# A fp32 hybrid decoder trunk on one core: first unit by pairs of feature tiles, substitution on GpSimd, gated rows at other ticks

## The chip, the cores and the metric

The kernel runs on one core of a Trainium2 chip, as one program. The metric is the device time of one execution in microseconds (us). The engines are named as in the profile: PE is TensorE (PEld its weight loads), DVE is VectorE, ACT is ScalarE, POOL is GpSimd, SP is SyncE.

## The reference, cut to what matters

Two layers on 256 tokens of width 1024, batch 1, all in float32. Each layer is half a SwiGLU feed-forward, a token mixer, cross-attention to 256 memory tokens and another half feed-forward, each behind an RMS norm. The first layer's mixer is windowed attention beside a linear recurrence; the second layer's is a gated DeltaNet of 8 heads of 128 in chunks, which needs the inverse of a unit triangular matrix for each chunk and head.

```python
def rmsnorm(x, g):
    return x * rsqrt(mean(x * x) + 1e-6) * g

def swiglu(h, w_in, w_out):
    gate, up = split(h @ w_in, 2)
    return (silu(gate) * up) @ w_out

for l in range(2):
    x = x + 0.5 * swiglu(rmsnorm(x, ffn1_norm[l]), ffn1_w_in[l], ffn1_w_out[l])
    x = x + mixer[l](rmsnorm(x, mix_norm[l]))           # l = 1: gated DeltaNet
    x = x + cross_attention(rmsnorm(x, xa_norm[l]), mem)
    x = x + 0.5 * swiglu(rmsnorm(x, ffn2_norm[l]), ffn2_w_in[l], ffn2_w_out[l])

# gated DeltaNet, per head and chunk: q, k, v through a causal convolution of four taps
# and silu; decay g = -exp(a_log) * softplus(a + dt_bias); c = cumsum(g)
A = tril(beta * (k @ k.T) * exp(c[:, None] - c[None, :]), -1)
T = inverse(I + A)            # by substitution
# u = T @ (beta v), w = T @ (beta exp(c) k); state from chunk to chunk; output gated by silu(z)
```

## The kernel before, in words

**Units.** The work is a list of products of activations by 256 columns of a weight matrix, 1024 rows deep: a *unit*. A unit's weights come as two *halves* of four 128-row tiles, 512 KB each, loaded by SP (`load_to`, L141) into one of five `raw` buffers. A half is split (`split_half`) into a high part (ACT copies it, rounded, L158) and a low part (DVE subtracts that from the original, L159), both in `wt`, of which four buffers hold two units. Each unit has two output groups of 128 columns. A group is eight high matmuls (L200, 512 moving columns: high and low activations) and eight low matmuls (L204, 256 columns), into one of three result banks `psw`, read back by ACT and DVE (L270, L271). So a bank is free again when DVE has done L271 for the group three before.

**What sets the order.** Each engine runs its instructions in one order, fixed at build time, and waits at the head of it. Outside the first units a scheduler makes that order from the order in which the code issues work. The code issues it in *ticks*: generators of work are advanced by `run`, and after each step `tick` splits the next half when a unit needs it, pops one step that was put off, adds one to `now`, and runs what `after(n, fn)` has made due. Tables of tick counts say when the steps of the DeltaNet mixer (`mixer1`) come: `EXP` for the exponentials of the decay, `INV` for the substitution, and others.

**The first units** are written out by hand under a manual schedule in `setup`. SP issues a norm's rows, then x in four pieces (feature tiles in pairs), with the first halves between. TensorE runs products of ones (`idle`), transposes x by pairs (L429), and ACT and DVE split the transposed x into high (L503) and low (L506). Then the products of units 0 and 1 follow by halves.

**The DeltaNet mixer.** Its units are, in this order: 'k0 k1 q0 q1 k2 v0 k3 v1 z0', then 'v3 z1 v2 q2' behind a first back substitution, 'q3', and 'z2 z3 K2 K3' behind the second. A unit such as k2 gives two heads (a *pair*, p = 0 to 3) of keys; DVE runs the convolution taps (`y`, L1081). The decay rows pass through memory (`gd`) and come back as `e` by POOL's transfers L1126, and ACT takes 16 exponentials (L1132), four a pair. DVE then makes the entries of the triangular blocks, `na` (L1176), which SP stores (L1180). For two pairs at a time (group 0: pairs 0, 1; group 1: pairs 2, 3) `invert` takes the 16 x 16 diagonal blocks back as `nb` (L1235), 64 of them side by side, and substitutes in 15 steps of a product (L1240) and a sum (L1242), on DVE. The finished blocks `ti` are copied transposed (L1244), stored (L1248) and read back spread over the partitions as `tu` (L1254); the function `back` goes on with products L1275 to L1287.

Small powers run on POOL (L341): `rs_dn` for the scale of keys and queries. The sums they need are products with ones on TensorE (L1110). L1204 is the product of keys and queries.

Of the kernel before, what the change touches and what calls it, by code (L numbers as in the profile page):

```python
# [9 lines left out]
F32 = mybir.dt.float32  # L10
# [3 lines left out]
AF = mybir.ActivationFunctionType  # L14
# [4 lines left out]
P = 128  # L19
S = 256  # L20
D = 1024
KD = 8
# [45 lines left out]
class Net:  # L68
    def __init__(self, tc, t):
        self.tc, self.nc, self.t = tc, tc.nc, t  # L70
        self.raws, self.halves = {}, {}
        self.plan = list(self.make_plan())
        self.queue = [(i, k) for i, u in enumerate(self.plan) for k in range(0, u[4], 4)]

        self.queue[1], self.queue[2] = self.queue[2], self.queue[1]
        self.n_load = self.n_half = self.n_take = 0
        self.later = deque()
        self.banks, self.n_bank = "w", 0
        self.now, self.due = 0, []
# [46 lines left out]
            yield from four("xa_wo", l)  # L126
            yield from ffn(2, l)

    def load_to(self, n, step=4):

        nc = self.nc
        while self.n_load < min(n, len(self.queue)):
            i, k = self.queue[self.n_load]
            name, l, c0, k0, nk, cols = self.plan[i]
            m = min(4, nk - k)
            raw = self.p_raw.tile([P, 4, 256], F32, name="raw")
            src = self.t[name][l, (k0 + k) * P:(k0 + k + m) * P, c0:c0 + cols]
            src = src.rearrange("(k p) c -> p k c", p=P)
            for u in range(0, m, step):
                us = slice(u, min(m, u + step))  # L140
                nc.sync.dma_start(raw[:, us, :cols], src[:, us])  # L141
            self.raws[self.n_load] = raw
            self.n_load += 1

    def split_half(self, step=4):

        nc = self.nc
        i, k = self.queue[self.n_half]
        name, l, _, _, nk, cols = self.plan[i]
        self.load_to(self.n_half + 1)  # L150
        n = min(4, nk - k)
        wt = self.p_wt.tile([P, 4, 2, 256], F32R, name="wt")
        raw = self.raws.pop(self.n_half)
        self.n_half += 1
        for u in range(0, n, step):
            us = slice(u, min(n, u + step))
            a, b, r = wt[:, us, 0, :cols], wt[:, us, 1, :cols], raw[:, us, :cols]
            nc.scalar.activation(a, r, AF.Copy)  # L158
            nc.vector.tensor_sub(b, r, a.bitcast(F32))  # L159
        self.halves.setdefault(i, []).append(wt)  # L160

    def w(self, name, c0):

# [23 lines left out]

    def mm3(self, out, wts, cols, mov, ks, k0=0, start=0, stop=KD):  # L190

        nc = self.nc
        for k in ks:
            i = k - k0
            w = wts[i // 4][:, i % 4]

            def high():
                nc.tensor.matmul(out.rearrange("p a s -> p (a s)"), w[:, 0, cols], mov[:, k].rearrange("p a s -> p (a s)"),  # L200
                                 start=k == start, stop=k == stop - 1)

            def low():
                nc.tensor.matmul(out[:, 0], w[:, 1, cols], mov[:, k, 0], start=False, stop=False)  # L204

            for part in (low, high) if k == stop - 1 else (high, low):
                part()

# [223 lines left out]
    def setup(self, ctx):  # L432
        nc, tc, t = self.nc, self.tc, self.t
# [20 lines left out]
        self.dcw = c.tile([P, P], F32, name="dcw")  # L454

        warm = c.tile([P, 1], F32, name="warm")
        nc.scalar.activation(warm, self.ones[:, :1], AF.Silu)
        x_pool = tc.tile_pool(name="xs", bufs=1, reuse_waits="tile")
        xs = x_pool.__enter__().tile([P, 2, D], F32, name="xs")
        x = t["x"][0].rearrange("(t p) d -> p t d", p=P)  # L460
        spare = self.p_sm.tile([P, S], F32, name="acc", bufs=2)
        rows0, rows, rows2 = self.dcw, spare[:, :P], spare[:, P:]

# [3 lines left out]
            eng.dma_start(dst[r0:r0 + n * times],  # L467
                          bass.AP(tensor=ap.tensor, offset=ap.offset, ap=[[0, times], [P, n], [1, P]]))

        put(rows0, 0, "ffn1_norm", nc.sync, times=8)  # L470

        for a, b in ((0, 256), (256, 512)):
            nc.sync.dma_start(xs[:, :, a:b], x[:, :, a:b])
        self.load_to(1, 2)
        self.load_to(2)
        for a, b in ((512, 768), (768, 1024)):
            nc.sync.dma_start(xs[:, :, a:b], x[:, :, a:b])
        self.load_to(RAW)
        xs = [xs[:, j] for j in range(2)]

# [5 lines left out]
        with tc.manual_schedule():  # L486

            def idle(n):
                ps = self.bank("w").rearrange("p a s -> p (a s)")
                for _ in range(n):  # L490
                    nc.tensor.matmul(ps[:, :P], self.ones, self.ones, start=True, stop=True)

            idle(7)
            gains = self.p_sm.tile([P, 1, S], F32, name="bc", bufs=2)[:, 0, :P]
            columns(gains, rows0, "w")
            banks = []

            def take(ks, ps):
                banks.append((ks, ps))
                g = lambda k: gains[:, C_FFN1 + k:C_FFN1 + k + 1]  # L500
                for j in range(2):
                    k = ks.start + j
                    nc.scalar.activation(self.x2[:, k, 0], ps[:, j], AF.Copy, scale=g(k))  # L503
# [8 lines left out]
            def products(u, half, j):  # L512
                self.mm3(self.first[u][j], self.halves[u], slice(j * P, j * P + P), self.x2,
                         range(4 * half, 4 * half + 4))

            self.transposed(xs, take, (0,))
            idle(3)
            self.transposed(xs, take, (1,))
            idle(6)
            self.split_half(2)  # L520
            products(0, 0, 0)
            self.split_half()
            products(0, 0, 1)
            self.transposed(xs, take, (2, 3))
            products(1, 0, 0)
            products(1, 0, 1)
            for u in range(2):
                self.split_half(2)
                for j in range(2):
                    products(u, 1, j)  # L530
# [477 lines left out]
    def mixer1(self, mid, kT_mem, mem_mov, gnext):  # L1008
# [4 lines left out]
        with tc.tile_pool(name="m1", bufs=1, reuse_waits="tile") as mp:  # L1013
# [213 lines left out]
            def invert(g):  # L1227
# [9 lines left out]

                def step(j):
                    n, m = 15 - j, j + 1
                    nc.vector.tensor_mul(tm[:, :n, :m], nb[:, j, m:, None].to_broadcast([64, n, m]),  # L1240
                                         ti[:, 0, j:m, :m].to_broadcast([64, n, m]))
                    nc.vector.tensor_add(ti[:, 0, m:, :m], ti[:, 0, m:, :m], tm[:, :n, :m])  # L1242
                    if j == 14:
                        nc.vector.tensor_copy(ti[:, 1], ti[:, 0].rearrange("p a b -> p b a"))  # L1244

# [147 lines left out]
            for i, part in enumerate(DN_ORDER):  # L1393
                if i % 2 == 0:
                    for step in part.split():
                        self.run(unit(step))
                    continue
                group, bg = part.split("|")
                gens = [back(int(p)) for p in group]
                bg = deque(unit(step) for step in bg.split())  # L1400
                parts = list(DN_FILL[i // 2])
                if i == 1:
                    self.fill(bg, 2)
                while gens:
                    gens = [g_ for g_ in gens if next(g_, 0) is None]
                    if gens:
                        self.fill(bg, parts.pop(0))
                if i == 1:
                    self.fill(bg)
                    for n, p in enumerate(group):  # L1410
                        self.after(1 + n, lambda p=int(p): gated(p))
                        self.after(4 + n, lambda p=int(p): gated_T(p))
                    continue
                for p in group:
                    gated(int(p))
                for p in group:
                    self.fill(bg, parts.pop(0))
                    gated_T(int(p))
                self.fill(bg)
# [81 lines left out]
```

## Time and profile before

| | us |
|---|---|
| median of 3 runs | 1252.54 (1251.08 to 1254.22) |
| profiled execution, its own time | 1250.74 |
| its span, first to last instruction | 1249.0 |
| TensorE busy | 1235.7 |
| VectorE busy | 929.3 |
| ScalarE busy | 751.8 |
| GpSimd busy | 80.9 |

The mean clock granted to TensorE was 0.999 of full speed. In rows of the profile, L12 is line 12 of the kernel; a tile's name is that of the program without its number. A row of the timeline gives the start in us, the time, engine, line, operation, output and inputs, shapes, how many operations are joined, and in brackets the idle time before it and what ended it. Busy time of different engines overlaps. SPq marks SP's issue of a transfer, not the transfer.

### The profile page before, as it was taken

The numbers are of one execution on the slowest core, as the hardware profiler recorded it, in microseconds if no ns is written. First come the engines' busy times: TensorE is split into PE (matmuls) and PEld (weight loads), VectorE is DVE, ScalarE is ACT, GpSimd is POOL, SyncE is SP. The second block draws the span as 40 slices with busy tenths as digits, with TensorE's granted clock in tenths as the row PEclk, the third lists the DMA queues.
The fourth block names the chain that finished last, engine by engine and source line by source line (L and its number), as shares of the span: only waits on it lengthen the run. The fifth ranks groups of instructions, "written<-read, shape, count | busy, mean of one in ns | idle before, by whom it ended". The sixth has DMA issues, their size and how long they took to land.

```text
span 1249.0 us, 20308 instructions
## 1 busy us (share of the span) xinstructions
PE 1235.7 (99%) x7702; PEld 1105.1 (88%) x7702; DVE 929.3 (74%) x1594; ACT 751.8 (60%) x1281; POOL 80.9 (6%) x97
## 2 busy tenths in 40 slices
PE   9999999999999999999999999999999999999998
PEld 8888889888998888888888888888898998888887
DVE  6987957788668778766877756989757668777753
ACT  7766545886555665545666544776757555665543
POOL 1000020000101000011000001020001101000000
PEclk9999999999999999999999999999999999999999
DMA  8766575534544565556656566667533545566552
GB/s 272 215 208 197 185 254 185 177 128 151 187 135 153 185 195 184 187 183 229 188 185 198 175 193 206 189 150 197 140 102 132 178 131 165 185 190 188 177 188 72
DMA packets 231018, 222.92 MB, mean 178 GB/s; under 512 B 14968, under 2 KB 228616, under 8 KB 230792
## 3 DMA queue, kind: packets, MB, share of 16 engines
q1 hardware_dynamic: 229448, 217.94, 55.9%
q0 software_dynamic: 1152, 3.15, 1.0%
q8 instruction: 60, 0.98, 0.3%
q10 hardware_dynamic: 320, 0.53, 0.1%
q14 instruction: 38, 0.31, 0.1%
HBM read 215.03 MB, written 5.51 MB: 177 GB/s over the span
## 4 chain that ended last, share of the span: by engine, by line
PE 90%; DVE 5%; ACT 2%; DMA 1%; issue 1%; POOL 1%; ACTq 0%; DVEq 0%; POOLq 0%
PE psw L200 21%; PE pss L200 16%; PE psw L204 11%; PE psf L200 11%; PE pss L204 8%; PE psf L204 5%; PE psw L242 5%; PE psf L242 4%; PE pss L242 3%; PE psw L216 2%; DVE wt L159 1%; PE psw L220 1%; ACT wt L158 1%; PE pss L1275 1%; PE psf L1281 1%
## 5 line engine op out<-in xcount | busy, mean ns | idle before, releaser
L159 DVE TENSOR_TENSOR wt<-raw,wt 128x1024 fp32r<-128x1024 f32 (+1 forms) x409 | 484.6, 1190 | 203.3 <-ACT wt L158 200.5
L158 ACT ACTIVATE wt<-raw 128x1024 fp32r<-128x1024 f32 (+1 forms) x409 | 418.6, 1031 | 172.3 <-PE psw L204 59.4
L200 PE MATMUL psw<-x,wt 128*128 128x512 f32 x864 | 310.6, 396 | 1.7 <-DVE xn L271 1.5
L204 PE MATMUL psw<-x,wt 128*128 128x256 f32 x864 | 224.9, 281 | 0.5 <-DVE wt L159 0.5
L200 PE MATMUL pss<-x,wt 128*128 128x512 f32 x520 | 187.4, 393 | 0.0
L200 PEld LDWEIGHTS psw<-x,wt 128*128 128x128 f32 x864 | 160.6, 188 | 29.7 <-issue 1.7
L204 PEld LDWEIGHTS psw<-x,wt 128*128 128x128 f32 x864 | 162.5, 188 | 9.4 <-DVE wt L159 1.0
L204 PE MATMUL pss<-x,wt 128*128 128x256 f32 x520 | 134.9, 280 | 0.0
L200 PE MATMUL psf<-x,wt 128*128 128x512 f32 x352 | 127.2, 394 | 0.0
L200 PEld LDWEIGHTS pss<-x,wt 128*128 128x128 f32 x520 | 97.7, 188 | 16.9 <-ACT bc L377 0.4
L204 PEld LDWEIGHTS pss<-x,wt 128*128 128x128 f32 x520 | 97.7, 188 | 5.4
L200 PE MATMUL psw<-h,wt 128*128 128x512 f32 x264 | 94.9, 396 | 0.0
L204 PE MATMUL psf<-x,wt 128*128 128x256 f32 x352 | 91.3, 280 | 0.0
L200 PE MATMUL pss<-h,wt 128*128 128x512 f32 x242 | 87.0, 396 | 0.0
L336 POOL TENSOR_TENSOR acc<-acc,sq 128x256 f32<-128x256 f32 x49 | 43.7, 891 | 658.5 <-ACT sq L334 557.5
L200 PEld LDWEIGHTS psf<-x,wt 128*128 128x128 f32 x352 | 66.1, 188 | 11.2
L204 PE MATMUL psw<-h,wt 128*128 128x256 f32 x264 | 72.0, 280 | 0.0
L204 PEld LDWEIGHTS psf<-x,wt 128*128 128x128 f32 x352 | 66.2, 188 | 3.5
L204 PE MATMUL pss<-h,wt 128*128 128x256 f32 x242 | 66.0, 280 | 0.0
L200 PEld LDWEIGHTS psw<-h,wt 128*128 128x128 f32 x264 | 49.6, 188 | 10.8
L200 PE MATMUL psf<-h,wt 128*128 128x512 f32 x154 | 55.4, 397 | 0.0
L200 PEld LDWEIGHTS pss<-h,wt 128*128 128x128 f32 x242 | 45.5, 188 | 9.8
(385 smaller groups left out, 2108.9 us busy)
## 6 DMA issues: line engine op xcount, KB each, us to landing
raw<-in_ffn_w_in_dram SPq DMA_DIRECT2D x175, 512.0 KB, 3.6
raw<-in_ffn_w_out_dram SPq DMA_DIRECT2D x80, 512.0 KB, 3.5
raw<-in_xa_wkv_dram SPq DMA_DIRECT2D x32, 512.0 KB, 3.4
raw<-in_dn_w_in_dram SPq DMA_DIRECT2D x32, 512.0 KB, 4.0
raw<-in_ab_w_in_dram SPq DMA_DIRECT2D x20, 512.0 KB, 3.5
raw<-in_xa_wq_dram SPq DMA_DIRECT2D x16, 512.0 KB, 3.5
raw<-in_xa_wo_dram SPq DMA_DIRECT2D x16, 512.0 KB, 3.3
raw<-in_ffn_w_out_dram SPq DMA_DIRECT2D x16, 256.0 KB, 2.7
```

Of the source, the lines that this page charges most:

```text
L158: nc.scalar.activation(a, r, AF.Copy)
L159: nc.vector.tensor_sub(b, r, a.bitcast(F32))
L200: nc.tensor.matmul(out.rearrange("p a s -> p (a s)"), w[:, 0, cols], mov[:, k].rearrange("p a s -> p (a s)"), start=k == start, stop=k == ...
L204: nc.tensor.matmul(out[:, 0], w[:, 1, cols], mov[:, k, 0], start=False, stop=False)
L216: nc.tensor.matmul(out.rearrange("p a s -> p (a s)"), mov[:, k, 0, tok], w.rearrange("p a s -> p (a s)"), start=k == 0, stop=k == KD - 1)
L220: nc.tensor.matmul(out[:, 0], mov[:, k, 1, tok], w[:, 0], start=False, stop=False)
L242: self.nc.tensor.matmul(out, a[u], b[w], start=first and i == 0, stop=last and i == 2)
L336: (eng or nc.gpsimd).tensor_add(self.acc, self.acc, sq)
L1275: nc.tensor.matmul(py[:, i], na[:, i], tu[:, 0, i], start=True, stop=True)
L1281: nc.tensor.matmul(pp[:, i], yy[:, i], tu[:, 1, i], start=True, stop=True)
```

## The change: what it does

It has four parts.

1. In the first unit, x and the weights are loaded alternately in pairs of feature tiles (`load_pair`), the norm's rows go to ACT's queue, the products of unit 0 go by pairs of tiles (four highs, then four lows), and the weights are split by pairs between the pieces of x. Eight idle products go.
2. The substitution's product and sum go from DVE to POOL. The copy behind them stays on DVE.
3. The gated rows and their transposes are put off by 2 + n and 6 + n ticks, not 1 + n and 4 + n.
4. `split_half` hands the splitting to `run`, as a generator. `run` calls `tick` after each step, so a split is a tick of its own: a unit in the steady part counts six ticks, before it counted four. The tables `EXP`, `INV` and the others keep their numbers.

```diff
-        self.queue[1], self.queue[2] = self.queue[2], self.queue[1]
...
+    def load_pair(self, n):
+        name, l, c0, _, _, cols = self.plan[0]
+        if n % 2 == 0:
+            self.raws[n // 2] = self.p_raw.tile([P, 4, 256], F32, name="raw")
+        src = self.t[name][l, 2 * n * P:(2 * n + 2) * P, c0:c0 + cols].rearrange("(k p) c -> p k c", p=P)
+        self.nc.sync.dma_start(self.raws[n // 2][:, 2 * n % 4:2 * n % 4 + 2, :cols], src)
+        self.n_load = n // 2 + 1
...
-    def split_half(self, step=4):
+    def split_half(self):
+        self.run(self.split_steps(4))
+
+    def split_steps(self, step):
...
             nc.scalar.activation(a, r, AF.Copy)
             nc.vector.tensor_sub(b, r, a.bitcast(F32))
-        self.halves.setdefault(i, []).append(wt)
+            yield
...
-        put(rows0, 0, "ffn1_norm", nc.sync, times=8)
-
-        for a, b in ((0, 256), (256, 512)):
-            nc.sync.dma_start(xs[:, :, a:b], x[:, :, a:b])
-        self.load_to(1, 2)
-        self.load_to(2)
-        for a, b in ((512, 768), (768, 1024)):
-            nc.sync.dma_start(xs[:, :, a:b], x[:, :, a:b])
+        put(rows0, 0, "ffn1_norm", nc.scalar, times=8)
...
+        for n in range(4):
+            nc.sync.dma_start(xs[:, :, n * 256:n * 256 + 256], x[:, :, n * 256:n * 256 + 256])
+            self.load_pair(n)
...
-            idle(7)
+            idle(5)
...
+            w0 = weights()
             self.transposed(xs, take, (0,))
             idle(3)
-            self.transposed(xs, take, (1,))
-            idle(6)
-            self.split_half(2)
-            products(0, 0, 0)
-            self.split_half()
-            products(0, 0, 1)
-            self.transposed(xs, take, (2, 3))
...
+            next(w0)
+            for n in range(3):
+                self.transposed(xs, take, (n + 1,))
+                products(0, range(2 * n, 2 * n + 2), late=True)
+                next(w0)
+            products(0, range(6, 8))
+            for half in range(2):
+                self.split_half()
+                products(1, range(4 * half, 4 * half + 4))
...
-                    nc.vector.tensor_mul(tm[:, :n, :m], nb[:, j, m:, None].to_broadcast([64, n, m]),
+                    nc.gpsimd.tensor_mul(tm[:, :n, :m], nb[:, j, m:, None].to_broadcast([64, n, m]),
                                          ti[:, 0, j:m, :m].to_broadcast([64, n, m]))
-                    nc.vector.tensor_add(ti[:, 0, m:, :m], ti[:, 0, m:, :m], tm[:, :n, :m])
+                    nc.gpsimd.tensor_add(ti[:, 0, m:, :m], ti[:, 0, m:, :m], tm[:, :n, :m])
...
-                        self.after(1 + n, lambda p=int(p): gated(p))
-                        self.after(4 + n, lambda p=int(p): gated_T(p))
+                        self.after(2 + n, lambda p=int(p): gated(p))
+                        self.after(6 + n, lambda p=int(p): gated_T(p))
```

Where the change moves instructions, the rows of the new order have the new program's line numbers, eleven or twelve above the old in the mixer (L1143 is the old L1132, L1255 the old L1244, L283 the old L271, L168 the old L159).

TensorE at the start of the program, before (L491 idle products of ones, L483 the norm's rows, L429 transposes of x, L200 and L204 high and low products):

```order
1 L491 MATMUL psw<-ones 128x128 x7
2 L483 MATMUL psw<-ident,dcw 128x128
3 L429 MATMUL psf<-ident,xs 128x128 x4
4 L491 MATMUL psw<-ones 128x128 x3
5 L429 MATMUL pss<-ident,xs 128x128 x4
6 L491 MATMUL psw<-ones 128x128 x6
7 L200 MATMUL psw<-x_79,wt 128x512
8 L204 MATMUL psw<-x_79,wt 128x256
```

and now:

```order
1 L500 MATMUL psw<-ones 128x128 x5
2 L492 MATMUL psw<-ident,dcw 128x128
3 L441 MATMUL psf<-ident,xs 128x128 x4
4 L500 MATMUL psw<-ones 128x128 x3
5 L441 MATMUL pss<-ident,xs 128x128 x4
6 L209 MATMUL psw<-x_79,wt 128x512 x4
7 L213 MATMUL psw<-x_79,wt 128x256 x4
8 L441 MATMUL psf<-ident,xs 128x128 x4
```

The first products stand right behind the second transposes, four highs and then four lows, and the next transposes stand between pairs.

ScalarE around the exponentials of the decay (e), in the units q1 and k2 of the mixer, before (th is the tanh or square of a finished convolution, xn the read of a result bank, wt a half's split):

```order
691 L158 ACTIVATE wt<-raw 128x4x256
692 L1078 ACTIVATE y<-xn,dcw 128x256
693 L1132 ACTIVATE e<-e,ngc 128x128 x3
694 L1087 ACTIVATE th<-y 128x512
695 L270 ACTIVATE xn<-psw 128x256
696 L1132 ACTIVATE e<-e,ngc 128x128 x3
697 L1104 ACTIVATE th<-y 128x512
```

and now:

```order
690 L1089 ACTIVATE y<-xn,dcw 128x256
691 L1143 ACTIVATE e<-e,ngc 128x128 x8
692 L1098 ACTIVATE th<-y 128x512
693 L282 ACTIVATE xn<-psw 128x256
694 L1143 ACTIVATE e<-e,ngc 128x128 x3
695 L1115 ACTIVATE th<-y 128x512
696 L1209 ACTIVATE q_8265<-y 128x256
697 L1089 ACTIVATE y<-xn,dcw 128x256
698 L1143 ACTIVATE e<-e,ngc 128x128 x5
699 L282 ACTIVATE xn<-psw 128x256
700 L167 ACTIVATE wt<-raw 128x4x256
```

Eight exponentials in a row stand ahead of the first th, and the split of v0's second half, which stood ahead of all exponentials, stands behind them.

VectorE around the copy of the finished blocks of group 0, in the new order (y taps of the convolution, wt splits of halves, ti the blocks):

```order
944 L1099 SCALAR_TENSOR_TENSOR y<-th,y 128x512
945 L1092 SCALAR_TENSOR_TENSOR y<-xn,dcw,y 128x254
946 L283 TENSOR_TENSOR xn<-psw,xn 128x256
947 L1092 SCALAR_TENSOR_TENSOR y<-xn,dcw,y 128x253
948 L1255 COPY ti<-ti 64x256
949 L168 TENSOR_TENSOR wt<-raw,wt 128x4x256
950 L1092 SCALAR_TENSOR_TENSOR y<-xn,dcw,y 128x255
951 L1124 TENSOR_SCALAR ss<-pss 128x4
952 L1092 SCALAR_TENSOR_TENSOR y<-xn,dcw,y 128x254
953 L283 TENSOR_TENSOR xn<-psw,xn 128x256
```

In the order before, the copy stood behind the split of v3's first half, four splits later, with the thirty operations of the substitution interleaved ahead of it; now it stands ahead of the split of v1's first half and of the eviction of v0's first result, and waits for GpSimd's thirty operations.

More of the change, by code (lines that the diff above doesn't have):

```diff
@@ L127, in make_plan, with load_to @@
             yield from ffn(2, l)
-    def load_to(self, n, step=4):
+    def load_pair(self, n):
[5 more added lines that the diff above has]
+        self.n_load = n // 2 + 1
+    def load_to(self, n):
         nc = self.nc
@@ L138, in load_to @@
             src = src.rearrange("(k p) c -> p k c", p=P)
-            for u in range(0, m, step):
-                us = slice(u, min(m, u + step))
-                nc.sync.dma_start(raw[:, us, :cols], src[:, us])
+            nc.sync.dma_start(raw[:, :m, :cols], src)
             self.raws[self.n_load] = raw
             self.n_load += 1
-    def split_half(self, step=4):
+    def split_half(self):
+        self.run(self.split_steps(4))
+    def split_steps(self, step):
         nc = self.nc
@@ L154, in split_half @@
         self.n_half += 1
+        self.halves.setdefault(i, []).append(wt)
         for u in range(0, n, step):
@@ L186, in after, with mm3 @@
         self.due.sort(key=lambda e: e[:2])
-    def mm3(self, out, wts, cols, mov, ks, k0=0, start=0, stop=KD):
+    def mm3(self, out, wts, cols, mov, ks, k0=0, start=0, stop=KD, only=""):
         nc = self.nc
@@ L204, in low @@
                 nc.tensor.matmul(out[:, 0], w[:, 1, cols], mov[:, k, 0], start=False, stop=False)
+            if only:
+                (high if only == "high" else low)()
+                continue
             for part in (low, high) if k == stop - 1 else (high, low):
@@ L456, in setup @@
         warm = c.tile([P, 1], F32, name="warm")
[L457 to L460, printed above, removed]
         spare = self.p_sm.tile([P, S], F32, name="acc", bufs=2)
@@ L468, in put @@
                           bass.AP(tensor=ap.tensor, offset=ap.offset, ap=[[0, times], [P, n], [1, P]]))
-        put(rows0, 0, "ffn1_norm", nc.sync, times=8)
-        for a, b in ((0, 256), (256, 512)):
-            nc.sync.dma_start(xs[:, :, a:b], x[:, :, a:b])
-        self.load_to(1, 2)
-        self.load_to(2)
-        for a, b in ((512, 768), (768, 1024)):
-            nc.sync.dma_start(xs[:, :, a:b], x[:, :, a:b])
+        put(rows0, 0, "ffn1_norm", nc.scalar, times=8)
+        nc.scalar.activation(warm, self.ones[:, :1], AF.Silu)
+        x_pool = tc.tile_pool(name="xs", bufs=1, reuse_waits="tile")
+        xs = x_pool.__enter__().tile([P, 2, D], F32, name="xs")
+        x = t["x"][0].rearrange("(t p) d -> p t d", p=P)
+        for n in range(4):
+            nc.sync.dma_start(xs[:, :, n * 256:n * 256 + 256], x[:, :, n * 256:n * 256 + 256])
+            self.load_pair(n)
         self.load_to(RAW)
@@ L510, in setup, with products, weights @@
             self.first = [[self.bank(w) for w in u] for u in ("ww", "ws")]
-            def products(u, half, j):
-                self.mm3(self.first[u][j], self.halves[u], slice(j * P, j * P + P), self.x2,
-                         range(4 * half, 4 * half + 4))
+            def products(u, ks, late=False):
+                js = [slice(j * P, j * P + P) for j in range(2)]
+                for which in ("high", "low") if late else ("",):
+                    for j in range(2):
+                        self.mm3(self.first[u][j], self.halves[u], js[j], self.x2, ks, only=which)
+            def weights():
+                for _ in range(2):
+                    yield from self.split_steps(2)
+            w0 = weights()
             self.transposed(xs, take, (0,))
             idle(3)
-            self.transposed(xs, take, (1,))
-            idle(6)
-            self.split_half(2)
-            products(0, 0, 0)
-            self.split_half()
-            products(0, 0, 1)
-            self.transposed(xs, take, (2, 3))
[L525 to L530, printed above, removed]
+            next(w0)
[7 more added lines that the diff above has]
+                products(1, range(4 * half, 4 * half + 4))
             self.load_to(4 + RAW)
```

## The prediction

> **What bounds the kernel now.** I read the page first, then a table of the engines by stretch, then what TensorE waits for, and last the order of events at two places: the first 13 us and the stretch from 805 to 860 us, where the delta mixer forms its decay and substitution. Two lines of the page, busy times and the chain of waits:
>
> ```profile
> PE 1235.7 (99%) x7702; PEld 1105.1 (88%) x7702; DVE 929.3 (74%) x1594; ACT 751.8 (60%) x1281; POOL 80.9 (6%) x97
> PE 90%; DVE 5%; ACT 2%; DMA 1%; issue 1%; POOL 1%; ACTq 0%; DVEq 0%; POOLq 0%
> ```
>
> TensorE is the bound nearly everywhere; a change can only shorten the rest or lengthen it. The table by stretch (first to last time; busy time of each engine) shows where the rest is:
>
> ```profile
> 0.00:25.00 25.00, 23.30 (x128) 20.34 (x129) 15.20 (x31) 16.77 (x31) 4.96 (x13) 1.00 0.82 261
> 25.00:775.00 750.00, 749.09 (x4546) 665.99 (x4544) 566.18 (x898) 445.48 (x715) 42.63 (x49) 1.00 0.59 187
> 800.00:825.00 25.00, 23.55 (x154) 21.01 (x153) 21.00 (x61) 17.44 (x40) 6.18 (x6) 1.00 0.73 178
> 825.00:850.00 25.00, 24.29 (x154) 21.18 (x154) 23.76 (x80) 21.10 (x48) 3.25 (x3) 1.00 0.53 140
> ```
>
> From 25 to 775 us TensorE lacks 0.9 us in all. In the delta mixer VectorE is nearly full: 23.76 of 25 us from 825 to 850. What TensorE waits for from 800 to 975 us (total, times, longest):
>
> ```profile
> PE psw L200 <- DVE xn L271: 1.5, 1, 1.5
> PE psf L200 <- DVE a L1357: 1.3, 1, 1.3
> PE pss L1355 <- DVE qk L1346: 1.0, 1, 1.0
> PE psw L216 <- DVE tm L1240: 0.4, 1, 0.4
> PE pss L1287 <- DVE tu L1282: 0.4, 1, 0.4
> PE psw L216 <- DVE xn L271: 0.3, 1, 0.3
> ```
>
> All six are waits for VectorE, 4.9 us together. That is what relief of VectorE could win.
>
> **The start (gain).** Rows of the first 13 us, TensorE, then SyncE, then ScalarE:
>
> ```profile
> 4.41 1.09 PE L429 MATMUL psf<-ident,xs 128*128 128x128 f32 x4
> 6.58 0.86 PE L429 MATMUL pss<-ident,xs 128*128 128x128 f32 x4
> 8.89 0.50 PE L200 MATMUL psw<-x,wt 128*128 128x512 f32 x1
> 9.88 0.39 PE L204 MATMUL psw<-x,wt 128*128 128x256 f32 x1 [0.50 <-DVE wt L159]
> 10.11 0.40 PE L200 MATMUL psw<-x,wt 128*128 128x512 f32 x1
> 10.46 0.40 PE L200 MATMUL psw<-x,wt 128*128 128x512 f32 x1
> 12.55 0.60 PE L429 MATMUL psf<-ident,xs 128*128 128x128 f32 x4
> 0.74 0.80 SPq L467 DMA_DIRECT2D dcw<-in_ffn_norm_dram  x1
> 1.59 0.92 SPq L473 DMA_DIRECT2D xs<-in_x_dram  x2
> 7.48 0.84 ACT L503 ACTIVATE x<-pss,bc 128x256 fp32r<-128x256 f32 x2 [1.10 <-PE pss L429]
> 8.21 1.15 ACT L158 ACTIVATE wt<-raw 128x512 fp32r<-128x512 f32 x2
> ```
>
> The norm's transfer leaves SyncE, so x is issued at 0.74, 0.85 us earlier. By pairs, the first product needs only x tiles 0 and 1 and one pair of weights, whose ScalarE copy (1.15 / 2 = 0.57) now stands ahead of the second pair of x. So it can follow the second transposes: if these end 0.5 us earlier, at about 6.9, instead of 8.89, that is 2.0 us. Some is given back: per pair ScalarE has 0.84 + 0.57 = 1.41, while TensorE has four highs and four lows, a pair of which takes 0.35 (10.11 to 10.46), 1.39, and four transposes at 0.60. VectorE's part of a pair (low weights and low x) follows ScalarE's and is longer than either: by about 0.1 to 0.2 us a pair TensorE catches up with it, and the last pair's low part waits, so 0.5 us is lost. I take -1.5. Bounds: -2.0 if nothing is given back; +1.0 if the fewer idle matmuls (eight less) leave TensorE slow for longer: four transposes took 1.09 and 0.86 early, 0.60 at 12.55, so two more such sets and slow products would cost about that.
>
> **A tick at every split.** The split of a half is now run through the routine that counts ticks, so a unit has six ticks, not four, and what is deferred by a count comes after two thirds as many units. In the long feed-forward stretches nothing waits on this: 0.9 us in 750 is all there was, bounded at ±0.5, taken as 0. The gated rows' counts grow from 1 and 4 to 2 and 6, which is two thirds of nearly the same place: 0, bounds ±1. In the delta mixer it moves three things: the decay rows (the transpose L1063 stands 14 product matmuls earlier), the exponentials and the substitution.
>
> **The exponentials (loss).** Rows around them, POOL, ScalarE, VectorE, TensorE:
>
> ```profile
> 811.22 3.66 POOL L1126 DMA_DIRECT2D e<-gd  x4 [0.71 <-DMA gd<-gt]
> 817.07 0.99 ACT L1132 ACTIVATE e<-e,ngc 128x128 f32<-128x128 f32 x3 [3.57 <-DMA e<-gd]
> 817.96 0.62 ACT L1087 ACTIVATE th<-y 128x512 f32<-128x512 f32 x1
> 819.46 0.69 ACT L1132 ACTIVATE e<-e,ngc 128x128 f32<-128x128 f32 x2 [0.32 <-DMA e<-gd]
> 818.61 0.69 DVE L1088 SCALAR_TENSOR_TENSOR y<-th,y 128x512 f32<-128x512 f32 x1 [0.36 <-ACT th L1087]
> 820.17 0.47 PE L200 MATMUL psw<-x,wt 128*128 128x512 f32 x1 [1.45 <-DVE xn L271]
> 822.45 1.14 PE L1204 MATMUL psf<-y 128*128 128x128 f32 x8
> ```
>
> ScalarE already stands 3.57 us before an e that a transfer has yet to bring. With the decay rows 14 x 0.174 = 2.4 us earlier (0.174 is half of the steady pair's 0.35), e arrives at 814.7 and the second head pair's at 816.7. But now eight exponentials, not three, stand ahead of th, and the split of v0's second half stands behind all sixteen. th is done at 816.7 + 4 x 0.33 + 0.62 = 818.6, the y from it at 819.3. TensorE's matmuls L1204, which read that y, now stand right behind unit k2's first group, not 24 product matmuls later. That group ended at about 815.1 (the wait ahead of 820.17 began at 818.7; a group of 16 is 2.78, and 0.8 of small matmuls lay in it). So TensorE stands about 4 us there, against 1.45 before. Carrying it on through the three result banks (k3's second group needs v0's first result evicted), that group begins at 834.1, worked out with the copy below, where before it began at 831.2 (820.17 + three groups of 2.78 + 2.7 of small matmuls): +2.9, even with a free substitution. I take +3; bounds 1.5 (half is made up) and 4.
>
> **The substitution on GpSimd (loss).** First, what it cost on VectorE, then the work ahead of it and the first of group 0, its copy at the end, and the second group's load and VectorE's wait for it:
>
> ```profile
> L1240 DVE TENSOR_TENSOR tm<-nb,ti x30: 156/199/218, 831.5 to 877.1; 64x15 f32<-64x15 f32 x4, 64x28 f32<-64x28 f32 x4, 64x39 f32<-64x39 f32 x4, 64x48 f32<-64x48 f32 x4
> 823.19 0.86 DVE L1176 SCALAR_TENSOR_TENSOR na<-psf,nb_all,e 128x128 f32<-128x128 f32 x3
> 826.37 0.61 SPq L1235 DMA_DIRECT2D nb<-d  x1
> 831.46 0.17 DVE L1240 TENSOR_TENSOR tm<-nb,ti 64x15 f32<-64x15 f32 x1
> 851.01 0.38 DVE L1244 COPY ti<-ti 64x256 f32<-64x256 f32 x1
> 861.77 0.60 SPq L1235 DMA_DIRECT2D nb<-d  x1
> L1240 DVEq EVENT_SEMAPHORE  x1: 21/21/21, 866.9 to 866.9; - x1
> ```
>
> Sixty operations of 0.2 us, 12 us of busy time, leave VectorE. What they cost on GpSimd no row shows; the nearest are these, an add of 256 elements on both engines, and the small powers:
>
> ```profile
> L336 POOL TENSOR_TENSOR acc<-acc,sq x49: 732/787/1395, 154.3 to 1058.5; 128x256 f32<-128x256 f32 x49
> L336 DVE TENSOR_TENSOR acc<-acc,sq x6: 417/422/426, 1196.8 to 1239.4; 128x256 f32<-128x256 f32 x6
> L341 POOL TENSOR_TENSOR rcol<-ms,mhalf x10: 549/714/1679, 21.1 to 1242.6; 128x2 f32<-128x2 f32 x8, 128x1 f32<-128x1 f32 x2
> ```
>
> Scaled by elements alone, 45 of 256 would be 0.13 us (4 us a group); by the power of one element, 0.55 (16 us). By the ratio of the adds, 787 / 422 = 1.87, the 0.2 become 0.37. Each waits for the one before. I take 0.33 each, 10 us a group, since an add is the nearer kind. The Trainium skill, "GPSIMD Engine Reference", section 3.1, gives 4497 against 2293 ns for an add of 2048, 1.96 times; as an estimate 0.39 each and 11.8 us a group, and the sum would end 2 us later. The trace's 1.87 agrees.
>
> The copy L1244 stays on VectorE, and in the new order it stands right behind the tap of k2's last part, ahead of the split of v1's first half and of the eviction of v0's first result. VectorE's work from the second na to the copy is 9 taps, 3 splits, 3 evictions and two larger operations, 9.3 us by spacings of 0.39, 1.13, 0.33 and 0.6, with about 1.3 of waits for ScalarE: from 820.3 (the last e at 818.0 and the operations ahead) to 831.2. Behind it the copy, a split, two taps, a sum and the eviction take 2.9: the 834.1 of above. The substitution can start when nb lands: before, na was done at 824.05 and nb issued 2.3 later; group 0's first operation began 5.1 after the issue, behind other work, and group 1's wait ended 5.1 after its issue. The landing takes 5.1 at most, and I take 4.4. So it starts at 820.3 + 2.3 + 4.4 = 827 and ends at 837: VectorE stands 6 us with work behind it for which TensorE waits, since k3's second group needs that eviction. TensorE had no slack left there (834.1 was VectorE's own pace), so +6. Bounds: 0 at 4 us a group, +12 at 16. On SyncE the stores L1248 and four loads of tu stand behind the copy, with only v3's second half between: that half is due some 17 us later, so nothing. On GpSimd the powers rs_dn of the later units queue behind the substitution; what reads them on VectorE stands behind the copy anyway: nothing.
>
> Group 1: from na of the fourth pair to the copy VectorE has four splits, two units, 11.3 us. The way through memory takes 2.3 + 5.1 and GpSimd 10: 17.4. VectorE stands 6 us, of which the three banks let TensorE run on for about one and a half groups, 4.5: +1.5. Bounds 0 and 6.
>
> Relief: of the six waits of TensorE, the first is in the exponentials' term, and 0.4 + 0.3 stood among the substitution's operations; with half of the 2.7 us behind, -1.5 (bounds 0 and -4). The way of the triangular factors to the back substitution is earlier by over 10 us, but that starts by its own count of units, so 0.
>
> **Sum.** -1.5 + 3 + 6 + 1.5 - 1.5 = +7.5. The profiled execution took 1250.74 us, 1.8 below the median of 1252.54; so 1258.2 against it, 1260 against the median.
>
> **Rivals.** *Relief wins* (faster): VectorE gets to the copy later than 834 because its own queue is late, or GpSimd needs under 0.2 us each, so the copy waits for nothing; 12 us leave the fullest engine, the waits for VectorE (4.9) go, and the start keeps 2.0: -6, 1246.5. For it: all six waits are VectorE's; against: a GpSimd add costs 1.87 of VectorE's. It decides at 7 us a group with the exponentials costing nothing. Chance 0.18. *A draw*: the substitution takes 5 us, the copy waits 1, relief and start pay for the exponentials: 1253; chance 0.2. *Contention*: GpSimd and VectorE slow each other, as the 1.395 of an add of mostly 0.787 hints (1.77 times); 17 us a group: 7 more at the first copy, 4 more at the second, so 1271; chance 0.14. The rule in the Trainium skill, "SBUF — State Buffer", section "SBUF: two separate sides", that a two-input VectorE operation and a GpSimd operation lock each other out for a whole instruction, would bring this; no row here shows whose lock the 1.395 was. My forecast has the remaining 0.48.
>
> **How the numbers follow.** About ±0.3% (3.75 us) can be told from no change. Slower takes the forecast and contention, 0.62; the draw gives same 0.2; relief gives faster 0.18. The range 1247 to 1270 reaches from the relief case to contention; the forecast's own is 1255 to 1266, from 7 to 14 us a group.
>
> **What would show it.** First product at about 7 us; TensorE idle near 815 to 819 before L1204; a wait of VectorE for GpSimd of about 6 us at the copy, TensorE idle behind it at k3; GpSimd operations of 0.3 to 0.35 us. Operations under 0.2 us, or no VectorE wait at the copy, make it wrong.

## The result and the profile after

The changed kernel takes 1271.46 us (1269.77 to 1272.05), the kernel before, beside it, 1253.37: the ratio is 1.0145, with a 95% interval of 1.0127 to 1.0163. It is slower by 18 us, where 7.5 were forecast; the range ended at 1270. The profiled execution took 1272.05 us, 21.3 over the profiled one of before. In the comparisons below, the kernel before took 1250.5 to 1254.0 us in executions with a mean granted clock of 0.999 or more and 1252.6 to 1259.0 us in those with less, so its median moves with their share.

The page's busy times, and the stretches (length; busy PE, PEld, DVE, ACT, POOL; granted clock; DMA) that changed:

```profile
PE 1242.2 (98%) x7686; PEld 1109.4 (87%) x7686; DVE 921.4 (73%) x1533; ACT 751.1 (59%) x1280; POOL 99.5 (8%) x157
...
800.00:825.00 25.00, 21.84 (x134) 19.04 (x133) 19.56 (x59) 18.33 (x45) 7.13 (x7) 0.93 0.68 158
825.00:850.00 25.00, 18.79 (x97) 16.20 (x96) 12.57 (x27) 11.73 (x21) 11.98 (x32) 0.73 0.60 155
875.00:900.00 25.00, 18.37 (x119) 16.78 (x118) 9.01 (x14) 8.97 (x16) 8.06 (x26) 0.86 0.34 84
```

TensorE does 97 matmuls from 825 to 850, before 154. And the granted clock, 1.00 in all these stretches before, is 0.73 to 0.93. The waits of TensorE from 795 to 980 us, and VectorE's largest from 795 to 900:

```profile
PE psf L1292 <- ACT yy L1288: 6.6, 1, 6.6
PE psw L209 <- DVE xn L283: 5.1, 1, 5.1
PE psf L1215 <- DVE y L1099: 2.8, 1, 2.8
PE psf L209 <- DVE a L1368: 1.6, 1, 1.6
PE pss L1121 <- ACT th L1115: 1.1, 1, 1.1
PE pss L1298 <- DVE tu L1293: 0.6, 1, 0.6
PE psf L1171 <- DVE y L1099: 0.4, 1, 0.4
PE psw L228 <- DVE xn L283: 0.3, 1, 0.3
...
DVE ti L1255 <- POOL ti L1253: 16.6, 2, 9.0
```

The third stands where the prediction put it, at the products of keys and queries behind k2's first group. TensorE's rows there show what follows a stop:

```profile
818.59 1.16 PE L1215 MATMUL psf<-y 128*128 128x128 f32 x8 [2.79 <-DVE y L1099]
819.58 1.00 PE L1121 MATMUL pss<-ones,th 128*128 128x1 f32 x8
820.44 0.69 PE L209 MATMUL psw<-x,wt 128*128 128x512 f32 x1
```

A high product takes 0.69, in place of 0.39: the granted clock is 0.50 from 820.53 (below). At the first copy (GpSimd, VectorE, TensorE):

```profile
826.46 0.38 POOL L1251 TENSOR_TENSOR tm<-nb,ti 64x15 f32<-64x15 f32 x1 [4.38 <-DMA nb<-d]
826.91 2.08 POOL L1253 TENSOR_TENSOR ti<-ti,tm 64x15 f32<-64x15 f32 x1
838.74 0.21 POOL L1253 TENSOR_TENSOR ti<-ti,tm 64x15 f32<-64x15 f32 x1
827.07 1.21 DVE L168 TENSOR_TENSOR wt<-raw,wt 128x1024 fp32r<-128x1024 f32 x1
828.21 0.68 DVE L1099 SCALAR_TENSOR_TENSOR y<-th,y 128x512 f32<-128x512 f32 x1
838.99 0.37 DVE L1255 COPY ti<-ti 64x256 f32<-64x256 f32 x1 [8.98 <-POOL ti L1253]
832.26 1.05 PE L1121 MATMUL pss<-ones,th 128*128 128x1 f32 x8 [1.09 <-ACT th L1115]
836.13 0.63 PE L209 MATMUL psw<-x,wt 128*128 128x512 f32 x1
841.88 0.76 PE L209 MATMUL psw<-x,wt 128*128 128x512 f32 x1 [5.12 <-DVE xn L283]
842.66 0.63 PE L209 MATMUL psw<-x,wt 128*128 128x512 f32 x1
843.30 0.63 PE L209 MATMUL psw<-x,wt 128*128 128x512 f32 x1
```

GpSimd needs 12.5 us for thirty operations, VectorE stands 9.0 at the copy, TensorE 5.1 for the eviction behind it, and then a pair of products takes 0.64 us, not 0.35. The clock had fallen already ahead of this stop: a high product takes 0.63 at 836.13, behind a wait of 1.1 us and eight products of one column. At the second copy (VectorE, ScalarE, ScalarE, TensorE):

```profile
885.12 0.37 DVE L1255 COPY ti<-ti 64x256 f32<-64x256 f32 x1 [7.62 <-POOL ti L1253]
886.50 0.63 ACT L1101 ACTIVATE y<-y 128x512 f32<-128x512 f32 x1 [7.96 <-DVE y L1092]
887.03 0.58 ACT L1288 ACTIVATE yy<-pss 128x512 f32<-128x512 f32 x1
887.66 2.08 PE L1292 MATMUL psf<-tu,yy 128*128 128x128 f32 x8 [6.63 <-ACT yy L1288]
```

ScalarE's silu waits for a convolution tap that stands behind the copy; behind the silu stands yy, a step of the back substitution, which TensorE needs. Last, the three stretches in which the clock record has half speed:

```profile
820.53:823.95 3.42, 3.42 (x12) 2.94 (x12) 3.15 (x8) 3.42 (x9) 1.22 (x1) 0.50 0.29 81
834.19:847.84 13.65, 8.53 (x30) 7.08 (x29) 6.23 (x14) 3.88 (x8) 4.94 (x15) 0.50 0.57 136
885.39:892.21 6.82, 4.55 (x17) 4.16 (x18) 2.76 (x6) 1.39 (x3) 0.00 (x0) 0.50 0.50 96
```

TensorE was busy 16.5 us in them; half of that, 8.2, is an estimate of the price of the clock. TensorE's busy time from 800 us to the end, before and then now, bears it out, with 7.7 us more for nearly the same matmuls:

```profile
800.00:1249.00 449.00, 438.59 (x2891) 397.43 (x2889) 325.21 (x614) 270.81 (x501) 32.13 (x34) 1.00 0.52 157
```

```profile
800.00:1269.90 469.90, 446.32 (x2887) 403.08 (x2885) 317.24 (x551) 271.33 (x502) 51.73 (x94) 0.97 0.50 150
```

The eight waits above are 18.5 us, the six of before in the same part of the program were 4.9, and the start is 0.9 us earlier: 18.5 - 4.9 + 8.2 - 0.9 = 20.9, where the two spans are 20.9 and the two profiled executions 21.3 us apart.

### The profile page after: what moved, and what is told of

It is laid out like the page before. It is cut to its first block, busy times and chain, and to the rows that moved or that the text cites. A ratio compares the mean times of both kernels' runs of the same rounds, so it can differ in the third digit from the quotient of the medians.

```text
span 1269.9 us, 20286 instructions
## 1 busy us (share of the span) xinstructions
PE 1242.2 (98%) x7686; PEld 1109.4 (87%) x7686; DVE 921.4 (73%) x1533; ACT 751.1 (59%) x1280; POOL 99.5 (8%) x157
## 5 line engine op out<-in xcount | busy, mean ns | idle before, releaser
L168 DVE TENSOR_TENSOR wt<-raw,wt 128x1024 fp32r<-128x1024 f32 (+1 forms) x408 | 484.6, 1192 | 204.1 <-ACT wt L167 201.7
L209 PE MATMUL psw<-x,wt 128*128 128x512 f32 x864 | 313.6, 401 | 5.4 <-DVE xn L283 5.1
L209 PEld LDWEIGHTS psw<-x,wt 128*128 128x128 f32 x864 | 162.7, 190 | 34.2 <-issue 5.6
L209 PE MATMUL pss<-x,wt 128*128 128x512 f32 x520 | 187.2, 393 | 0.0
L213 PEld LDWEIGHTS psw<-x,wt 128*128 128x128 f32 x864 | 164.2, 191 | 9.3 <-DVE wt L168 0.7
L209 PE MATMUL psf<-x,wt 128*128 128x512 f32 x352 | 127.1, 394 | 0.0
L209 PEld LDWEIGHTS pss<-x,wt 128*128 128x128 f32 x520 | 97.6, 188 | 16.5
L209 PE MATMUL psw<-h,wt 128*128 128x512 f32 x264 | 94.9, 396 | 0.0
L209 PE MATMUL pss<-h,wt 128*128 128x512 f32 x242 | 87.0, 396 | 0.0
L209 PEld LDWEIGHTS psf<-x,wt 128*128 128x128 f32 x352 | 66.1, 188 | 11.2
L209 PEld LDWEIGHTS psw<-h,wt 128*128 128x128 f32 x264 | 49.6, 188 | 10.8
L209 PE MATMUL psf<-h,wt 128*128 128x512 f32 x154 | 55.4, 397 | 0.0
L209 PEld LDWEIGHTS pss<-h,wt 128*128 128x128 f32 x242 | 45.5, 188 | 9.8
```

## The experiments

| run | us | ratio to the kernel before (95%) | granted clock |
|---|---|---|---|
| changed kernel | 1271.46 | 1.0145 (1.0127 to 1.0163) | 0.990 |
| e1 substitution on VectorE | 1260.49 | 1.0066 (1.0045 to 1.0086) | 0.995 |
| e2 copies on GpSimd too | 1258.76 | 1.0051 (1.0034 to 1.0068) | 0.995 |
| e3 no ticks in a split | 1265.03 | 1.0097 (1.0077 to 1.0116) | 0.994 |
| e4 the start alone | 1253.31 | 0.9998 (0.9985 to 1.0011) | 0.999 |
| e5 e2 without ticks | 1256.94 | 1.0027 (1.0015 to 1.0039) | 0.996 |
| e6 e2, TensorE kept busy | 1263.50 | 1.0074 (1.0050 to 1.0098) | 0.996 |
| e7 half of the steps | 1262.97 | 1.0064 (1.0042 to 1.0086) | 0.995 |
| e8 e4, norm on SyncE (one run) | 1255.70 | - | 0.998 |
| e9 e5, rq_all on GpSimd | 1257.15 | 1.0026 (1.0012 to 1.0039) | 0.995 |
| e10 e9 with the old start | 1258.12 | 1.0032 (1.0020 to 1.0044) | 0.996 |
| e11 e1, TensorE kept busy | 1255.77 | 1.0017 (1.0003 to 1.0032) | 1.000 |
| e12 second group alone on GpSimd | 1252.95 | 1.0001 (0.9987 to 1.0015) | 0.999 |
| e13 TensorE kept busy at the second copy | 1268.93 | 1.0112 (1.0094 to 1.0131) | 0.994 |
| e14 second copy alone on GpSimd | 1262.39 | 1.0058 (1.0040 to 1.0075) | 0.993 |

The kernel before came out between 1252.0 and 1255.6 in the different comparisons, so the steps below are taken from the ratios; where medians are compared, the text says so.

**e1 to e4: the parts apart.**

```diff
e1 (to the changed kernel)
-                    nc.gpsimd.tensor_mul(tm[:, :n, :m], ...
-                    nc.gpsimd.tensor_add(ti[:, 0, m:, :m], ...
+                    nc.vector.tensor_mul(tm[:, :n, :m], ...
+                    nc.vector.tensor_add(ti[:, 0, m:, :m], ...
e2 (to the changed kernel)
-                        nc.vector.tensor_copy(ti[:, 1], ...
+                        nc.gpsimd.tensor_copy(ti[:, 1], ...
e3 (to the changed kernel); e4 is e3 with e1's edit
-        self.run(self.split_steps(4))
+        for _ in self.split_steps(4):
+            pass
...
-                        self.after(2 + n, ... gated(p))
-                        self.after(6 + n, ... gated_T(p))
+                        self.after(1 + n, ... gated(p))
+                        self.after(4 + n, ... gated_T(p))
```

> The changed kernel with the sixty operations of the substitution back on VectorE; start, ticks and gated rows stay changed. Queue theory (VectorE stands at the copy behind GpSimd, and what it holds up costs about 19 of the 18 to 21 us; ticks cost 2 to 3 at the exponentials; start wins 0.9): 1253 to 1257. Tick theory (the earlier places of the mixer's steps cost most): 1264 or more. Contention theory (GpSimd's work slows its neighbours): 1253 to 1257 too; the next run tells it from the queue.

> The changed kernel with the transposed copy of the finished blocks also on GpSimd, so that no instruction of VectorE waits for the substitution; the sixty operations stay on GpSimd. Queue theory: both waits of VectorE (9.0 and 7.6 us) go, 1253 to 1257, and TensorE's clock no longer falls after a stop of 5 to 6 us. Contention theory: 1265 or more, with VectorE's two-input operations longer beside GpSimd. Tick theory: 1264 or more.

> The changed kernel with the split of a half no longer counting ticks, and the gated rows at their old counts; start and GpSimd's substitution stay changed. Queue theory: the copy still stands ahead of other work on VectorE by the planner's estimate of GpSimd, so part of the wait stays: 1258 to 1268. Tick theory: 1252 to 1255.

> Only the new start: the substitution on VectorE, no ticks in a split, gated rows at their old counts. All theories: the traces of before and after differ by 0.9 us once the first units are done, so 1252 to 1253, 0.5 to 1.3 us under the kernel before.

e4 gained nothing that can be measured, where 0.5 to 1.3 us were expected; e3 lies in the range of the queue theory. e1 and e2 lie 2 to 4 us above it and below the others'. Read as steps: the start 0.0%; the ticks, and the gated rows with them (e1 less e4), 0.68%, 8.5 us; the substitution moved, with nothing of VectorE waiting at a copy (e2 less e1), -0.15%, -1.9 us; the copies left on VectorE (changed kernel less e2) 0.94%, 11.8 us. Each of these differences is uncertain by about 0.25%. So the copies are the largest part, and beside a substitution on VectorE the ticks cost more than the 2 to 3 us of my expectation. The parts don't simply add, though: the same ticks cost 0.48%, 6.0 us, in the changed kernel (less e3) and 0.24%, 3.0 us, in e2 (less e5 below), and the copies cost 0.70%, 8.8 us, without the ticks (e3 less e5).

**e6, e11, e13: the clock by itself.** Products of ones, whose results are overwritten, are added where TensorE stood: 14 ahead of the products of pair 0 (e11 to e1, e6 to e2), 24 at the second copy (e13).

```diff
e6, e11
+                    for i in range(14 if p == 0 else 0):
+                        nc.tensor.matmul(kq[:, i % 4], self.ones, self.ones, start=True, stop=True)
e13
+                    for i in range(24 if p == 1 and b == 5 else 0):
+                        nc.tensor.matmul(pp[:, i % 4], self.ones, self.ones, start=True, stop=True)
```

> The run with the substitution on VectorE and ticks in the splits (1260.49), with 14 products of ones where TensorE stood 3.2 us before the products of keys and queries of pair 0. Clock theory: the 3.4 us of half clock at 820.7 do not come, 1 to 3 us less: 1257 to 1260, and the granted clock of that stretch is 1.00. If only the stop counts: 1260 to 1262.

> The changed kernel, with 24 products of ones on TensorE where it stood 6.6 us behind the second copy (ahead of the second pair's products L1292, into the bank that these overwrite); nothing else is added. Clock theory: the half clock from 885.4 to 892.2 does not come; TensorE was busy 4.55 us in it, so 2.3 us less: 1268 to 1270 where the changed kernel gives 1271.5. If the clock costs nothing: 1271 to 1273.

> The run with the copy on GpSimd (1258.76), and ahead of the products of keys and queries of pair 0, where TensorE stood 3.2 us and its clock then ran at half for 10.2 us, 14 products of ones, about 3 us of work whose results are overwritten. Clock theory (the stop itself costs under half; half of 10 us of slow clock is 5): 1253 to 1257 although work is added. If the slow clock costs nothing: 1259 to 1262.

e11 is 4.7 us faster than e1 by the medians (6 by the ratios, uncertain by 3), though it computes more. The stretch from 800 to 825 us of e1, then of e11:

```profile
800.00:825.00 25.00, 21.43 (x132) 18.77 (x132) 19.14 (x58) 18.34 (x45) 7.14 (x7) 0.93 0.66 154
```

```profile
800.00:825.00 25.00, 23.48 (x163) 20.97 (x162) 19.68 (x58) 18.66 (x46) 6.92 (x7) 1.00 0.67 158
```

The clock stays at 1.00 there, and through the rest of the mixer, where e1 had two more stretches of 3.4 us at half. In e1's three slow stretches TensorE was busy 10.2 us, so as an estimate 5.1 of the 8.5 us are slow clock. e13 took 2.5 us off the changed kernel by the medians, as expected. Its stretch behind the second copy, the products of ones and the wait that is left:

```profile
875.00:900.00 25.00, 23.68 (x184) 22.40 (x184) 9.67 (x17) 9.95 (x24) 6.54 (x23) 1.00 0.31 73
...
878.99 5.52 PE L1292 MATMUL psf<-ones 128*128 128x128 f32 x48
885.83 1.16 PE L1294 MATMUL psf<-tu,yy 128*128 128x128 f32 x8 [1.32 <-ACT yy L1288]
```

VectorE waits there as before, and the clock is 1.00, not 0.86. But the gain has two parts: TensorE reached this stop 1.9 us earlier than in the changed kernel (the products L1294 ahead of it began at 878.10, there L1292 at 879.98): ahead of it its slow stretches were 6.8, 3.4 and 3.4 us, not 3.4 and 13.7, and its stop at the first copy was 2.6 us, not 5.1, though nothing was edited there. It left the stop 3.9 us earlier (the first L209 behind it began at 892.22, not at 896.14). So the edit itself is worth about 2.0 us; why the rest came at the first copy the record does not show. e6 missed: its clock stayed at 1.00 from 800 to 825, but it came out 4.7 us slower than e2 by the medians. The scheduler's order changed: VectorE now came to a power behind GpSimd's queue earlier and stood 7.8 us for it, not 4.1 (the part on e5 below), TensorE stood 7.3 us, and its clock fell there.

**e7 and e14: the length of the wait.** e7 leaves out 7 of the 15 steps of each substitution (so it does not compute the inverse); e14 moves only the second group's copy.

```diff
e7
-                    self.after(t1 + j // 3, lambda j=j: step(j))
+                    if j % 2 == 0:
+                        self.after(t1 + j // 3, lambda j=j: step(j))
e14
-                        nc.vector.tensor_copy(ti[:, 1], ...
+                        (nc.gpsimd if g else nc.vector).tensor_copy(ti[:, 1], ...
```

> The changed kernel with 7 of the 15 steps of each substitution left out (16 operations a group on GpSimd, not 30; the inverse is then not the reference's). Queue theory: VectorE's stand at the copies falls from 9.0 and 7.6 us to about 4 and 2, and the time to 1261 to 1264 (by 7 to 10 us); if GpSimd's length did not set it: 1269 to 1272.

> The changed kernel with the second group's copy alone on GpSimd; the first stays on VectorE. If the stand at the second copy is the cause of the 8 us that the traces show there: 1262 to 1265. By the prediction's term for it: 1270.

With 16 operations a group VectorE waits 6.9 us at the two copies in place of 16.6, and the time falls by 8.5 us by the medians. e14 falls by 9.1 us by the medians, 0.87% or 10.9 us by the ratios: in its trace neither the wait of TensorE behind the second copy nor the slow stretch there comes, so the stand at the second copy is the cause. It keeps VectorE's stand of 9.4 us and TensorE's of 5.7 at the first copy, and is slower than e2, where the first copy's stand is gone as well, by 0.07% in the ratios, 3.6 us in the medians and 5.1 us in the profiled executions. In e2 VectorE stands 4.1 us for a power behind GpSimd's queue instead, and the slow stretch behind the exponentials lasts 10.2 us, not 3.4. So the price of the first copy stays open: up to 5 us, and by the ratios nothing that can be told.

**e5, e9, e10, e12: is there a place for the substitution on GpSimd?** Here nothing counts a tick more than before. e5 has substitution and copy on GpSimd, e9 the scale rq_all too, e10 the same with the old start, e12 is the kernel before with only the second group and its copy on GpSimd.

```diff
e9 (to e5), e10
-                    self.after(1, lambda: nc.vector.tensor_scalar(rq_all[:, :, hs], ...
+                    self.after(1, lambda: nc.gpsimd.tensor_scalar(rq_all[:, :, hs], ...
e12 (to the kernel before)
+                    eng = nc.gpsimd if g else nc.vector
-                    nc.vector.tensor_mul(tm[:, :n, :m], ...
-                    nc.vector.tensor_add(ti[:, 0, m:, :m], ...
+                    eng.tensor_mul(tm[:, :n, :m], ...
+                    eng.tensor_add(ti[:, 0, m:, :m], ...
```

> Start changed; the substitution and its copy both on GpSimd; splits count no ticks and the gated rows have their old counts. If the two losses are additive (ticks 7 us, VectorE's stand at the copy 12), and the substitution on GpSimd is worth the 1.7 us between the last two runs: 1251 to 1253, no slower than the kernel before. If the lock between GpSimd's and VectorE's operations costs by itself: 1256 or more.

> The run with substitution and copy on GpSimd and no ticks (1256.94 against 1254.43), with the scale rq_all, which VectorE stood 6.7 us for behind GpSimd's queue (TensorE 6.0 of them), also on GpSimd. Queue theory: no instruction of VectorE that others need soon waits for GpSimd, so 5 to 6 us go and 12 us of VectorE's work are away: 1249 to 1252 where the kernel before gives 1253 to 1254. If the lock between the two engines costs by itself: still 2 us or more over the kernel before.

> The kernel before with only these three on GpSimd (substitution, copy, rq_all): old start, old ticks. If the new start wins 0.9 us: that much over the last run; if its gain is given back by later weights, as the run with the start alone suggests: the same within 0.5 us.

> The kernel before with only the second group's substitution and its copy on GpSimd; the first group's stay on VectorE, where powers for the scales of later units would queue behind it on GpSimd (VectorE stood 4.7 and 8.0 us for such a power in the last two runs with all on GpSimd). Queue theory: no power is due beside the second group, so nothing waits, and the six microseconds of VectorE's work beside it were mostly hidden: the kernel before less 0 to 1.5 us. If any substitution on GpSimd costs by itself: 1 us or more over the kernel before.

e5, e9 and e10 stay 0.26 to 0.32% slower. VectorE's rows of e5 and then of e9 show what it waits for:

```profile
845.43 0.17 DVE L1214 TENSOR_SCALAR rq_all<-rs_dn 128x4 f32<-128x4 f32 x1 [6.67 <-POOL rs_dn L354]
```

```profile
846.18 0.16 DVE L1165 TENSOR_TENSOR hb_all<-ss,rs_dn 128x4 f32<-128x4 f32 x1 [4.73 <-POOL rs_dn L354]
```

The power rs_dn runs on GpSimd, behind the thirty operations. With rq_all moved away, the next reader, hb_all, waits. TensorE stood 6.0 us in e5 and 3.1 in e9 for a split of VectorE's behind these. My forecasts for e5, e9 and e10 were wrong: I had taken away one reader, not the queue. By their times alone, e5 and e9 would also fit a cost of GpSimd's and VectorE's operations on each other; no run here separates that beside the first group. Between e9 and e10, the start is worth nothing that can be told. e12, where no power is due beside the second group, is the same as the kernel before (1.0001): GpSimd's substitution costs nothing there that can be told, and VectorE's relief wins nothing. No version beat the kernel before by more than can be told.

**e8: the norm's rows back on SyncE.** One edit to e4: nc.scalar to nc.sync for those rows.

> Only the new start, with the norm's rows back on SyncE ahead of x. In the run with the new start alone TensorE waited 0.8 us for those rows, which ScalarE's queue brought late. If that eats the start's gain: the first product earlier by 0.3 to 0.8 us than 8.1, and the first units' end with it. If x issued 0.85 us later costs as much: the same within 0.3 us.

TensorE waited 0.8 and 0.7 us for x in place of 0.8 for the norm, and its first product came at 8.37, not at 7.42. So neither forecast held: the first product came later. It is one run, and in its mixer TensorE had a stop of 2.5 us and a slow stretch of 3.4 that e4 had not, so it decides nothing on the total. TensorE's first four highs in it took longer than the 1.20 of the changed kernel; why, no row shows:

```profile
8.37 2.06 PE L210 MATMUL psw<-x,wt 128*128 128x512 f32 x4
```

## Why the prediction was wrong, step by step

**What failed: the price of a stop of TensorE.** Every term of the sum priced a stop by its length. The clock was named only for the start (its bound of +1.0). In the changed kernel three stretches at half speed, 24 us together, cost about 8.2 us; e11 shows that they don't come where the stop is filled, and e13 shows it for the second copy. Between the profiled executions the change was +21.3 where +7.5 was forecast: the clock is 8.2 of the 13.8 us that were missing, and most of the rest is the second copy, below.

**The exponentials, +3 with bounds 1.5 and 4.** The mechanism was right: the stop ahead of the products of keys and queries was there, 2.8 us, behind eight exponentials, and VectorE came to the first copy at 830.0, where I had 831.2 (the list of VectorE's work in the prediction adds up to 830.7). As waits it cost about what was forecast: 2.8 and 1.1 us where 1.5 stood. The whole price was not in the sum: the ticks cost 3.0 to 8.5 us, depending on what stands beside them (the steps above), and 4.7 of the 8.5 go when TensorE is kept busy (e11).

**The first copy, +6.** VectorE's stand was 9.0, not 6, since GpSimd took 12.5 us and not 10, and VectorE came 1.2 us earlier. TensorE's wait behind it was 5.1, near the 6 forecast. The operations were nearly as I had them, the product and then the sum (shortest, median and longest in ns):

```profile
L1251 POOL TENSOR_TENSOR tm<-nb,ti x30: 207/280/791, 826.5 to 884.6; 64x15 f32<-64x15 f32 x4, 64x28 f32<-64x28 f32 x4, 64x39 f32<-64x39 f32 x4, 64x48 f32<-64x48 f32 x4
L1253 POOL TENSOR_TENSOR ti<-ti,tm x30: 211/296/2075, 826.9 to 884.9; 64x15 f32<-64x15 f32 x4, 64x28 f32<-64x28 f32 x4, 64x39 f32<-64x39 f32 x4, 64x48 f32<-64x48 f32 x4
```

A product at 0.28, a sum at 0.30 and 0.08 between are 0.36 each, where 0.33 was taken. What came on top was one sum of 2.08 beside VectorE's split and y: that looks like the contention of the third rival, for one operation of the first group and not for all.

**The second copy, +1.5 with bounds 0 and 6.** TensorE stood 6.6 us, not 1.5. By e14 the second copy cost 9 to 11 us, what the clock adds included (about 2.0 of them, by e13). The step that failed was the cover of 4.5 us from the three result banks: it was reckoned for the products of units, but ScalarE's silu waited for a tap behind the copy, and yy behind the silu. I had looked for what stands behind the waiting instruction on VectorE, and not for what then stands behind it on ScalarE.

**GpSimd's queue, nothing.** In the changed kernel that held, because the copy waited as long. With the copies on GpSimd it was the next wait (e5, e9).

**The start, -1.5.** First products came at 8.09, not 6.9. ScalarE's queue brought the norm's rows late:

```profile
0.74 1.26 ACTq L475 DMA_DIRECT2D dcw<-in_ffn_norm_dram  x1
5.01 0.45 PE L492 MATMUL psw<-ident,dcw 128*128 128x128 f32 x1 [1.46 <-DMA dcw<-in_ffn_norm_dram]
8.09 1.20 PE L209 MATMUL psw<-x,wt 128*128 128x512 f32 x4
```

The read of unit 3's second result came 0.9 us earlier than before (33.02 against 33.91); with the start alone nothing is left (e4).

**Relief, -1.5.** The parts that the prediction names, 0.7 and half of 2.7, add to 2.0 and not to 1.5. e2 less e1 is -1.9 us: the size forecast, though less than these comparisons can tell from nothing, and e12 shows none for the second group.

The time came within a microsecond of the contention rival's 1271, but by luck and not by its way: the two substitutions took 12.5 and 11.8 us, not 17.

## What to carry to other kernels

Price a stop of TensorE by its length and by the slow stretch behind it, half of TensorE's busy time until the clock is back: 13.6 us of added waits came here with about 8 us of slow clock. When work moves to a free engine, list every short operation that the slow chain now holds up in that engine's queue, and every reader of its last result, and follow the wait through two engines, not one. Work moved off an engine that is nearly full wins only what TensorE waited for it, and here that was less than could be told.

## What the runs showed of the hardware

Stops of TensorE of 2.8 us (changed kernel), 3.2 (e1) and 2.0 (e9) were followed by half clock for 3.4 or 6.8 us; stops of 1.45 (before), 2.0 (e5) and 2.1 (e12) were not: at 2 us it went either way. The length of the one stop does not decide alone. In the changed kernel the second slow stretch began at 834.19, behind a wait of 1.1 us and products of one column, and the 5.1 us stop (836.76 to 841.88) came when the clock was down already. In each trace all edges of slow stretches lie whole multiples of 3.41 us apart (in the changed kernel 820.53, 823.95, 834.19, 847.84, 885.39 and 892.21). On that grid the stop of e9 (817.63 to 819.64) lies within one step, 817.52 to 820.94, while those of e5 (818.67 to 820.64) and e12 (818.88 to 820.98) have an edge of theirs inside, at 819.61 and 819.37 (counted back from the edges at 846.92 and 1246.03). That fits, but no run here tests it. The Trainium skill, "TensorE: Matmul & The Clock Gate", in "Part 1: The HAM clock gate", puts the fall after at least one idle window of about 3.4 us; the length of the slow stretches, 3.4 us or multiples, agrees with such a window, but here stops shorter than it were enough.

GpSimd's sum of 2.08 us ended at 828.99, right after two operations of VectorE that read two tensors (827.07 to 828.89). This agrees with the rule cited in the prediction from the Trainium skill, "SBUF — State Buffer": one waits out the other. By the record the sum that waited had begun first, at 826.91. In e2, where VectorE went on working beside it, sums of 1.2 to 1.5 us came three times in the first group, and its substitution took 14.7 us.
